# Splitting the transposed residual at the layer borders: four scaled blocks kept in fp32, then one rounding and one remainder over 512 columns

## The chip, the cores and the metric

The kernel runs on one core of a Trainium2 chip. The core has a matrix engine (TensorE, PE in the rows, with PEld for its weight loads), VectorE (DVE), ScalarE (ACT), GpSimd (POOL) and a queue engine that issues the DMAs (SP). Each engine works through its own list of instructions in order, and waits on semaphores of the others. The metric is the device time of one execution in microseconds; a change of under about 0.2% can't be told from none.

## The reference

Two transformer stacks, one after the other, on 256 tokens of width 1024, all in fp32. What matters here is the frame: each layer normalises the residual `x`, multiplies it by learned weights `g`, and feeds it to large matrix products.

```python
def rmsnorm(x, g, eps):                       # g: (1024,)
    return x * rsqrt(mean(x * x, -1) + eps) * g

for layer in range(2):                        # first block
    x = x + mixer(rmsnorm(x, ln1_g[layer])) @ w_o[layer]          # three attention mixers
    x = x + square(relu(rmsnorm(x, ln2_g[layer]) @ w_up[layer])) @ w_down[layer]
x = rmsnorm(x, final_g)
for i in range(4):                            # second block: retention, conformer, short conv, retention
    h = mixer_i(rmsnorm(x, norm_g[i, 0]))
    x = x + rmsnorm(h, norm_g[i, 1])
    h = square(relu(rmsnorm(x, norm_g[i, 2]) @ w1[i])) @ w2[i]
    x = x + rmsnorm(h, norm_g[i, 3])
```

Retention also multiplies its gated output by weights `ret_gn_g` before `ret_w_out`.

## The kernel before

All 256 tokens stay on chip as two tiles `x0` and `x1` of 128 tokens by 1024 (called token half 0 and 1 below). Weights stream in by DMA, 512 KB at a time, into `raw` buffers. To multiply with near-fp32 precision, each operand is split in two parts of the type fp32r: `hi`, the value rounded to fp32r by ScalarE, and `lo`, the remainder `value - hi` by VectorE. A product then is three matmuls: hi·hi, hi·lo, lo·hi. For weights these parts are `whi` and `wlo` (a 128x1024 cast on ScalarE and a 128x1024 subtraction on VectorE for each 512 KB). For the activations they are tiles named `t4k` in the rows.

A *border* is the place between one sub-layer and the next: six mixers and six MLPs give eleven borders, and the input adds one at the start. At a border the class `Pre` takes the new residual. `Pre.split` (line 661) transposes four 128x128 blocks of `x` on TensorE into one PSUM bank (`ps<-ident,x` in the rows) and calls `split_scaled` (line 905), which makes the hi and lo parts of `x` transposed times `g`. `g` lies along the partitions there, so each of the four blocks has its own column of the tile `cv`, and ScalarE's scale takes one column at a time. A border calls `split_scaled` four times: two token halves by two column halves of 512. The retention mixer calls it too, eight times in each of its two layers (`do_g`, twice for each of four heads). That makes 12 × 4 + 16 = 64 calls.

After a border the next sub-layer's first products run in a special order (`lagged`, line 814): with the order `LAG`, token half 0 first, its 16 matmuls with hi over all eight blocks, then its 8 with lo, then the same 24 for token half 1. Before the border, `tail` (line 883) finishes the last products of token half 0 ahead of those of token half 1, so that the residual of half 0 can be finished while TensorE still works on half 1.

The program is first recorded and then put in order by a list scheduler (`Rec.schedule`, line 411): each engine takes, among the instructions whose inputs its cost figures hold ready, the one with the earliest due time, and the due times are counted back from TensorE's order. So a change in one helper moves instructions on every engine near it. The order so found is the order that each engine then keeps on the chip. In the trace all instructions have one line (L563), and go by the names of their tiles.

Of the kernel before, what the change touches and what calls it, by code (L numbers as in the profile page):

```python
# [15 lines left out]
AF = mybir.ActivationFunctionType  # L16
ALU = mybir.AluOpType

P = 128
# [680 lines left out]
class Net:  # L700
# [204 lines left out]
    def split_scaled(self, pt, hi, lo, t, col):  # L905
        nc = self.nc
        ts_ = slice(t * P, (t + 1) * P)
        bs = [(b, self.cv[:, col + b:col + b + 1], pt[:, b * P:(b + 1) * P]) for b in range(4)]
        for b, g, src in bs:
            nc.scalar.activation(hi[:, b, ts_], src, AF.Copy, scale=g)  # L910
        for b, g, src in bs:
            nc.vector.scalar_tensor_tensor(lo[:, b, ts_], src, g, hi[:, b, ts_], op0=ALU.mult, op1=ALU.subtract)

    def evac(self, dst, src):
        self.flip ^= 1
# [863 lines left out]
```

## Time and profile before

| | |
|---|---|
| runs | 1937.51 us median of 3 (1935.68 to 1938.13) |
| profiled execution | 1934.96 us, its span 1933.2 us |
| TensorE busy | 1894.6 us (98%), mean granted clock 0.992 |
| VectorE busy | 1696.6 us (88%), 2895 instructions |
| ScalarE busy | 1249.6 us (65%), 2165 instructions |
| GpSimd busy | 155.6 us (8%) |

The span is from the first to the last instruction; 1.8 us of the profiled execution lie around it. Busy time is the union of an engine's instructions. Matmuls overlap in TensorE's pipeline: one with 512 columns is listed with some 0.39 us, while the next starts 0.23 us after it. The mean of one ScalarE or VectorE instruction also holds an overlap with the next one of about 0.1 us.

### The profile page before, as it was taken

What the parts mean: (1) busy time and instruction counts of PE and PEld (TensorE: products, weight loads), DVE (VectorE), ACT (ScalarE), POOL (GpSimd) and SP (SyncE); (2) the same over time, 40 slices, a digit from 0 to 9 for tenths busy, and PEclk for the clock granted to TensorE, in tenths of its full rate; (3) what the DMA queues carried; (4) which work ended last, traced back from release to release, by engine and by line L of the source; (5) the groups of instructions that cost most, each with busy time, mean ns of one, the idle gap of its engine ahead of it and who ended that gap; (6) DMA issues with size and microseconds to landing.
All of it is one profiled execution on the core that took longest, in us unless ns stands there. A gap on an engine that the chain in (4) does not pass through costs nothing.

```text
span 1933.2 us, 31326 instructions
## 1 busy us (share of the span) xinstructions
PE 1894.6 (98%) x11444; PEld 1675.7 (87%) x11444; DVE 1696.6 (88%) x2895; ACT 1249.6 (65%) x2165; POOL 155.6 (8%) x233
## 2 busy tenths in 40 slices
PE   8999999999999999999998899999999999999998
PEld 7989998888997888899978789979899889888997
DVE  7879999789999776699989899987799987758998
ACT  7557776557776335577679677664676753546775
POOL 2200002110001000000039300000000010000000
PEclk9999999999999999999999899999999999999999
DMA  6345656244565555455642456656456655553563
GB/s 232 113 151 179 210 199 201 77 156 162 198 223 204 180 173 181 135 184 198 229 137 102 131 167 208 208 181 220 135 190 217 208 197 171 169 183 131 192 212 120
DMA packets 95771, 341.49 MB, mean 177 GB/s; under 512 B 10624, under 2 KB 10880, under 8 KB 95616
## 3 DMA queue, kind: packets, MB, share of 16 engines
q1 hardware_dynamic: 95616, 339.49, 52.9%
q8 instruction: 89, 1.46, 0.3%
q14 instruction: 66, 0.54, 0.1%
HBM read 338.40 MB, written 1.05 MB: 176 GB/s over the span
## 4 chain that ended last, share of the span: by engine, by line
PE 90%; DVE 5%; ACT 2%; issue 1%; DMA 1%; POOL 1%; DVEq 0%; POOLq 0%; ACTq 0%
PE ps L563 90%; DVE wlo L563 2%; DVE s2k L563 1%; ACT s2k L563 1%; DVE ps L563 1%; POOL col L563 1%; DMA raw<-in_w 1%; DVE x L563 0%; ACT whi L563 0%; DVE raw L563 0%; DVE t4k L563 0%; DMA x<-in_x 0%; DVE r2k L563 0%; DVE s1k L563 0%; ACT t4k L563 0%
## 5 line engine op out<-in xcount | busy, mean ns | idle before, releaser
L563 ACT CAST whi<-raw 128x1024 fp32r<-128x1024 f32 (+2 forms) x807 | 779.8, 991 | 424.6 <-PE ps L563 237.8
L563 DVE TENSOR_TENSOR wlo<-raw,whi 128x1024 fp32r<-128x1024 f32 (+2 forms) x807 | 913.2, 1156 | 126.2 <-ACT whi L563 122.2
L563 PE MATMUL ps<-whi,t4k 128*128 128x512 f32 (+2 forms) x2808 | 882.0, 392 | 8.4 <-ACT t4k L563 6.7
L563 PE MATMUL ps<-t4k,whi 128*128 128x256 f32 x3712 | 661.9, 282 | 0.0
L563 PEld LDWEIGHTS ps<-whi,t4k 128*128 128x128 f32 x2808 | 523.2, 189 | 115.3 <-ACT t4k L563 9.0
L563 PEld LDWEIGHTS ps<-t4k,whi 128*128 128x128 f32 x3712 | 571.6, 188 | 8.9
L563 PE MATMUL ps<-wlo,t4k 128*128 128x512 f32 (+2 forms) x1404 | 532.3, 392 | 0.0
L563 PE MATMUL ps<-t4k,wlo 128*128 128x256 f32 x1856 | 510.4, 281 | 0.0
L563 PEld LDWEIGHTS ps<-t4k,wlo 128*128 128x128 f32 x1856 | 345.0, 189 | 0.1
L563 PEld LDWEIGHTS ps<-wlo,t4k 128*128 128x128 f32 x1404 | 265.4, 190 | 48.3 <-DVE wlo L563 0.4
L563 DVE TENSOR_TENSOR raw<-raw,raw 128x1024 f32<-128x1024 f32 (+1 forms) x168 | 159.3, 948 | 0.4
L563 POOL TENSOR_TENSOR col<-col,mhalf 128x1 f32<-128x1 f32 (+1 forms) x48 | 43.5, 915 | 1137.9 <-DVE col L563 1137.6
L563 ACT ACTIVATE s2k<-ps 128x512 f32<-128x512 f32 (+2 forms) x116 | 67.2, 582 | 88.6 <-PE ps L563 87.8
L563 DVE TENSOR_TENSOR t4k<-s2k,t4k 128x512 fp32r<-128x512 f32 (+1 forms) x172 | 106.0, 616 | 6.4 <-ACT t4k L563 6.1
L563 ACT CAST t4k<-s2k 128x512 fp32r<-128x512 f32 (+1 forms) x172 | 97.0, 564 | 2.3 <-DVE s2k L563 1.3
L563 ACT ACTIVATE s2k<-s2k 128x512 f32<-128x512 f32 (+1 forms) x118 | 73.9, 627 | 27.5 <-DVE s2k L563 27.1
L563 PE MATMUL ps<-s2k,s2k 128*128 128x64 f32 (+6 forms) x492 | 85.1, 309 | 6.6 <-DVE s1k L563 6.0
L563 PEld LDWEIGHTS ps<-s2k,s2k 128*128 128x128 f32 (+2 forms) x492 | 72.0, 198 | 18.3 <-DVE s1k L563 6.4
L563 PE MATMUL ps<-whi,r2k 128*128 128x512 f32 x288 | 85.4, 395 | 0.2 <-DVE s2k L563 0.2
L563 DVE SCALAR_TENSOR_TENSOR t4k<-ps,cv,t4k 128x128 fp32r<-128x128 f32 x256 | 72.0, 342 | 11.7 <-ACT t4k L563 11.5
L563 ACT ACTIVATE t4k<-ps,cv 128x128 fp32r<-128x128 f32 x256 | 71.4, 378 | 13.0 <-PE ps L563 8.2
L563 DVE TENSOR_TENSOR s2k<-s2k,s2k 128x128 f32<-128x128 f32 (+1 forms) x200 | 68.4, 346 | 3.7 <-ACT s2k L563 3.7
(119 smaller groups left out, 1276.4 us busy)
## 6 DMA issues: line engine op xcount, KB each, us to landing
raw<-in_w SPq DMA_DIRECT2D x599, 512.0 KB, 4.2
raw<-in_w SPq DMA_DIRECT2D x26, 384.0 KB, 3.6
row<-in_rows SPq DMA_DIRECT2D x11, 512.0 KB, 5.8
raw<-in_w SPq DMA_DIRECT2D x8, 288.0 KB, 3.0
raw<-in_w SPq DMA_DIRECT2D x4, 432.0 KB, 7.0
kcs<-in_kc SPq DMA_DIRECT2D x2, 768.0 KB, 7.8
x<-in_x SPq DMA_DIRECT2D x4, 256.0 KB, 6.1
out_dram<-x SPq DMA_DIRECT2D x4, 256.0 KB, 2.0
```

The lines of the kernel that those rows point to most:

```text
L563: op.dma = fn(*[res(a) for a in op.args], **{k: res(a) for k, a in op.kw.items()})
```

## The change

`split_scaled` is the only function changed. ScalarE's four scaled copies go into a new fp32 tile `w` in SBUF (128x512, tag `s2k`) instead of rounding straight into `hi`. Then the existing helper `hilo` makes both parts: one ScalarE cast of 512 columns rounds `w` into `hi`, and one VectorE subtraction of 512 columns writes `w - hi` into `lo`. Before, VectorE formed the remainder by four instructions that each read the PSUM block, `g` and `hi`.

```diff
@@ split_scaled
         bs = [(b, self.cv[:, col + b:col + b + 1], pt[:, b * P:(b + 1) * P]) for b in range(4)]
+        w = self.t("s2k", [P, 4, P])
         for b, g, src in bs:
-            nc.scalar.activation(hi[:, b, ts_], src, AF.Copy, scale=g)
-        for b, g, src in bs:
-            nc.vector.scalar_tensor_tensor(lo[:, b, ts_], src, g, hi[:, b, ts_], op0=ALU.mult, op1=ALU.subtract)
+            nc.scalar.activation(w[:, b, :], src, AF.Copy, scale=g)
+        self.hilo(hi[:, :, ts_], lo[:, :, ts_], w)
```

```python
    def hilo(self, hi, lo, src):
        self.nc.scalar.copy(hi, src)
        self.nc.vector.tensor_sub(lo, src, hi)
```

The first place is ScalarE's order at the border from the second MLP to the first retention layer, token half 0. Before (`ps_330` and `ps_174` hold the transposed column halves, `t4k_181` and `t4k_122` are their hi parts, `s2k<-x` are sums of squares):

```order
L563 ACTIVATE s2k_116,col_163<-x_65 128x512
L563 ACTIVATE s2k_410,col_282<-x_65 128x512
L563 ACTIVATE t4k_181<-ps_330,cv 128x128 x4
L563 ACTIVATE t4k_122<-ps_174,cv 128x128 x4
L563 CAST whi_127<-raw_98 128x1024
```

ScalarE's order at the same place in the change (`s2k_89` and `s2k_168` are the new fp32 tiles, `t4k_190` and `t4k_1519` the hi parts):

```order
L563 ACTIVATE s2k_89,col_266<-x_65 128x512
L563 ACTIVATE s2k_168,col_578<-x_65 128x512
L563 ACTIVATE s2k_89<-ps_139,cv 128x128 x4
L563 ACTIVATE s2k_168<-ps_165,cv 128x128
L563 CAST t4k_190<-s2k_89 128x4x128
L563 ACTIVATE s2k_168<-ps_165,cv 128x128 x3
L563 CAST whi_347<-raw_96 128x1024
L563 CAST t4k_1519<-s2k_168 128x4x128
```

Each column half's hi part is now written by a cast after its four copies, and the cast of the first stands behind the first copy of the second.

The second place is TensorE's order at the border from the first retention mixer to its MLP, around the transposes of token half 1 (`x_65`). Before (`ps_114` collects half 0's first products, with lo parts in `t4k_129` and `t4k_122`; `ps_330` collects those of half 1, with hi part `t4k_337`):

```order
L563 MATMUL ps_483<-ident,x_65 128x128 x4
L563 MATMUL ps_114<-whi_613,t4k_129 128x512
L563 MATMUL ps_174<-ident,x_65 128x128 x4
L563 MATMUL ps_114<-whi_613,t4k_129 128x512
L563 MATMUL ps_114<-whi_520,t4k_129 128x512 x2
L563 MATMUL ps_114<-whi_266,t4k_122 128x512 x2
L563 MATMUL ps_114<-whi_155,t4k_122 128x512 x2
L563 MATMUL ps_330<-whi_613,t4k_337 128x512
```

TensorE's order there in the change (half 0 in `ps_320`, half 1 in `ps_451` with hi part `t4k_332`):

```order
L563 MATMUL ps_320<-whi_194,t4k_341 128x512 x2
L563 MATMUL ps_320<-whi_126,t4k_341 128x512 x2
L563 MATMUL ps_320<-whi_531,t4k_196 128x512
L563 MATMUL ps_451<-ident,x_65 128x128 x4
L563 MATMUL ps_320<-whi_531,t4k_196 128x512
L563 MATMUL ps_175<-ident,x_65 128x128 x4
L563 MATMUL ps_320<-whi_251,t4k_196 128x512 x2
L563 MATMUL ps_451<-whi_194,t4k_332 128x512
```

Between the last transposes and half 1's first product stood seven matmuls, and there now stand two.

## Rows read from the trace of the kernel before

**Rows 1.** The page: busy time of each engine, then the chain by engine.
```profile
PE 1894.6 (98%) x11444; PEld 1675.7 (87%) x11444; DVE 1696.6 (88%) x2895; ACT 1249.6 (65%) x2165; POOL 155.6 (8%) x233
...
PE 90%; DVE 5%; ACT 2%; issue 1%; DMA 1%; POOL 1%; DVEq 0%; POOLq 0%; ACTq 0%
```

**Rows 2.** Waits of all engines: waiting engine and its output, releaser: total us, times, longest.
```profile
PE ps L563 <- DVE s1k L563: 6.9, 2, 6.0
...
PE ps L563 <- ACT t4k L563: 6.7, 5, 1.9
...
PEld ps L563 <- DVE wlo L563: 0.4, 1, 0.4
```

**Rows 3.** Timeline, TensorE and ScalarE, MLP to retention: start us, us, what, [idle].
```profile
606.35 1.32 PE L563 MATMUL ps<-ident,x 128*128 128x128 f32 x8 [1.10 <-DVE x L563]
609.59 0.50 PE L563 MATMUL ps<-whi,t4k 128*128 128x512 f32 x1 [1.92 <-ACT t4k L563]
...
609.19 2.14 ACT L563 ACTIVATE t4k<-ps,cv 128x128 fp32r<-128x128 f32 x8
```

**Rows 4.** Timeline, TensorE and ScalarE: MLP to conformer, then MLP to short conv.
```profile
986.31 0.80 PE L563 MATMUL ps<-whi,t4k 128*128 128x512 f32 x1 [1.62 <-ACT t4k L563]
...
1285.68 0.80 PE L563 MATMUL ps<-whi,t4k 128*128 128x512 f32 x1 [1.16 <-ACT t4k L563]
```

**Rows 5.** Timeline, ScalarE and TensorE, MLP to the second retention.
```profile
1556.46 1.64 ACT L563 ACTIVATE t4k<-ps,cv 128x128 fp32r<-128x128 f32 x6
...
1555.19 0.47 PE L563 MATMUL ps<-whi,t4k 128*128 128x512 f32 x1
...
1556.87 0.50 PE L563 MATMUL ps<-whi,t4k 128*128 128x512 f32 x1 [0.51 <-ACT t4k L563]
...
1557.89 0.40 PE L563 MATMUL ps<-whi,t4k 128*128 128x512 f32 x1
```

**Rows 6.** Windows, attention border, retention: stretch, length, PE, PEld, DVE, ACT, POOL, clock.
```profile
125.00:145.00 20.00, 20.00 (x99) 16.33 (x98) 14.99 (x28) 10.84 (x25) 0.00 (x0) 1.00 0.24 81
...
730.00:805.00 75.00, 75.00 (x341) 61.11 (x340) 46.04 (x68) 38.96 (x67) 0.35 (x1) 1.00 0.55 176
```

**Rows 7.** Lines by shape: busy us, mean ns of one, idle before.
```profile
L563 DVE SCALAR_TENSOR_TENSOR t4k<-ps,cv,t4k 128x128 fp32r<-128x128 f32 x256 | 72.0, 342 | 11.7 <-ACT t4k L563 11.5
L563 ACT ACTIVATE t4k<-ps,cv 128x128 fp32r<-128x128 f32 x256 | 71.4, 378 | 13.0 <-PE ps L563 8.2 <-DVE t4k L563 3.6
L563 DVE TENSOR_TENSOR t4k<-s2k,t4k 128x512 fp32r<-128x512 f32 x88 | 60.0, 682 | 6.4 <-ACT t4k L563 6.1
...
L563 ACT CAST t4k<-s2k 128x512 fp32r<-128x512 f32 x88 | 54.1, 615 | 2.1 <-DVE s2k L563 1.3
```

**Rows 8.** Timeline, ScalarE: the first four copies, at the program's start.
```profile
5.50 1.14 ACT L563 ACTIVATE t4k<-ps,cv 128x128 fp32r<-128x128 f32 x4 [0.51 <-PE ps L563]
```

**Rows 9.** Timeline, ScalarE and TensorE, retention to its MLP, token half 1.
```profile
813.68 2.17 ACT L563 ACTIVATE t4k<-ps,cv 128x128 fp32r<-128x128 f32 x8 [1.71 <-DVE t4k L563]
...
813.05 0.60 PE L563 MATMUL ps<-ident,x 128*128 128x128 f32 x4
...
813.72 0.60 PE L563 MATMUL ps<-ident,x 128*128 128x128 f32 x4
814.08 2.11 PE L563 MATMUL ps<-whi,t4k 128*128 128x512 f32 x8
```

**Rows 10.** Timeline, TensorE, conformer to its MLP; the wait for token half 1.
```profile
1114.69 0.63 PE L563 MATMUL ps<-ident,x 128*128 128x128 f32 x4 [1.14 <-DVE x L563]
```

**Rows 11.** Windows: clock after two waits, clock at 1556, the conformer's convolution.
```profile
610.70:614.10 3.40, 3.40 (x14) 2.66 (x13) 3.40 (x11) 3.40 (x11) 0.39 (x1) 0.50 0.82 269
...
1283.10:1289.90 6.80, 5.64 (x20) 4.19 (x19) 6.36 (x14) 5.71 (x20) 1.58 (x1) 0.50 0.58 213
...
1556.00:1560.00 4.00, 3.49 (x16) 2.53 (x15) 4.00 (x9) 3.08 (x11) 1.46 (x1) 1.00 0.18 46
...
994.00:1062.00 68.00, 61.54 (x424) 57.23 (x422) 62.18 (x126) 60.87 (x142) 56.60 (x75) 0.97 0.30 101
```

## Prediction

> **What bounds the kernel now.** I read the shares of busy time and the chain that ended last first. TensorE is busy 98% of the span and makes 90% of the chain; VectorE, at 88%, makes 5% [rows 1]. So time can be lost or won only where TensorE stands still, and I went on to the waits. TensorE waits for hi parts of activations (`t4k` from ScalarE) five times, 6.7 us in all. Its weight loads wait for `wlo`, VectorE's main product, once, for 0.4 us; the longest wait for VectorE is one of 6.0 us, inside the conformer, at a tile named `s1k` that the change doesn't touch [rows 2]. VectorE is full but runs ahead of TensorE almost everywhere.
>
> Then the timelines of the borders. They fall into three kinds. At the four borders from an MLP to a retention, conformer or short-conv mixer TensorE has nothing to do between the transposes and the first product: it waits 1.92 us at 609.59 and restarts 0.40 us after ScalarE's first copy at 609.19, since the first product needs one block of hi alone [rows 3]; at two others it waits 1.62 and 1.16 us [rows 4]; at the fourth it starts early with four matmuls on two blocks, waits 0.51 us and goes on [rows 5]. At the borders from a mixer to its MLP, TensorE has products of token half 0 left while half 1's hi parts are made. At the three attention borders and in the retention mixers' interior it has more than enough: 20.00 of 20.00 us and 75.00 of 75.00 us busy [rows 6].
>
> **The change part by part.** Engine time first. Of the 256 remainders on VectorE, 72.0 us go; 64 subtractions of 0.682 us, 43.6 us, come: -28.4 us. ScalarE keeps its 256 copies, now to fp32, which I cost the same, and gets 64 casts of 0.615 us: +39.4 us [rows 7]. ScalarE is busy 65% [rows 1], so nothing follows from its sum alone; on DMAs and on GpSimd the change puts nothing, and no row shows TensorE waiting there at these places. The new tile takes a buffer from `s2k`'s pool; I cost that at nothing, because at these places the pool's other users have finished, and half a microsecond at most per border if not, about one cast.
>
> [...]
>
> Now the delay of hi. Before, the first product could start 0.40 us after the first copy. In the order of the change the cast stands behind the four copies and the first copy of the other column half, so five copies at 0.25 us each (four take 1.14 us, the last of them about 0.38, hence 0.25 from start to start [rows 7, 8]), then 0.615 us of cast, and 0.06 us for two handovers: 1.93 us. So hi of the first half comes 1.5 us later, and nothing of it can be used before.
>
> Uncovered borders: at 609, 986 and 1285 that is 1.5 us each, 4.5 us. At 1556 ScalarE has made two copies early and starts the other six at 1556.46; three of these come ahead of the cast, so hi is ready at 1556.46 + 0.75 + 0.615 + 0.05 = 1557.88. By then TensorE has now done eight matmuls, four from 1555.19 and four from 1556.87; the ninth starts at 1557.89 [rows 5]. Eight times 0.23 us is 1.9 us that now come after. Sum 6.4 us.
>
> Half-covered borders, retention to its MLP: ScalarE starts when the transposes of half 1 at 813.05 end, at 813.68 [rows 9], and hi comes 1.93 us later, at about 815.6. In the new order TensorE has left from 813.65 on only one matmul (0.23 us), the second four transposes (0.36 us, from 813.72 to 814.08 [rows 9]) and two matmuls, in sum 1.0 us: it waits about 1.0 us. Before, the seven matmuls in that place made the wait none. The second retention's border has the same two matmuls left, 1.0 us; the short conv's has one left instead of five, 1.1 us. Sum 3.1 us. The five matmuls that are missing there are done earlier, in time in which TensorE was busy anyway, so they don't pay the wait back.
>
> Conformer to its MLP: TensorE already waits 1.14 us, for VectorE's `x` [rows 10]. Ahead of that `x` stand eight remainders, now two subtractions: 8 × 0.281 - 2 × 0.682 = 0.9 us [rows 7] that VectorE may give back, against 1.5 us of later hi: between +0.6 and +1.5, taken +1.0. Start of the program: the copies at 5.50 [rows 8] are followed by the first weights' casts on the same engine, so one cast, 0.6 us (bounds 0 and 1.2, two casts). Attention borders and retention's interior: nothing, hidden by products of the other half; without that cover the three borders and sixteen calls would cost 1.5 us each, 28 us, which I leave out, as TensorE shows no gap there [rows 6].
>
> The clock. [...] A stretch of 3.4 us at half the clock holds 1.7 us of work at the full one, so it costs 1.7 us. At 1556, after a wait of 0.72 and then of 0.51 us, the clock stays 1.00. There the stop becomes one of over 2 us in a piece, as long as the one before 609.59, so I expect it to fall: +1.7, but with a chance of some 6 in 10: +1.0. Bounds for all borders: -0.8 each (a stretch that is slow already is in part spent idle) and +1.7 each.
>
> VectorE's relief. 28.4 us less work helps only where TensorE waits on VectorE. By rows 2 the wait on `wlo` is worth 0.4 us. The waits inside the conformer, where VectorE has work for 62.18 of 68 us [rows 11], may shrink by what the border ahead gives back: 16 × 0.281 - 4 × 0.682 = 1.8 us. I take -1.5 in all, with bounds 0 and -6 (1.8 at three borders where VectorE holds up `x`).
>
> Sum: 6.4 + 3.1 + 1.0 + 0.6 + 1.0 - 1.5 = 10.6 us. The profiled execution took 1934.96 us, its span 1933.2 and 1.8 around it; with 10.6 that is 1945.6. The median of the runs shown is 2.55 us above it (1937.51), so 1948 us.
>
> **The rivals.** B, no change: a new order is made for the new instruction lengths, and the stalls are refilled. TensorE's weight parts are ready ahead, so leftover products of the mixer, moved behind the transposes, could hide what I count at 815 and its like; and the four uncovered waits could hide behind casts that stand there anyway. Against it: the order of the change shows fewer such products, not more, and at 609 none are left. It would leave 4.5 us at three borders and take back 1.5 to 4 of it: +2, 1939.5 us.
>
> C, faster: VectorE's backlog decides. For it: 88% busy, and the wait of 6.0 us on `s1k` [rows 2] after a stretch where VectorE is nearly full [rows 11]. Then 1.8 us at each of three borders and 0.9 at the conformer's exit come back, 6.3 us, the delay of hi costs 1 to 2, and the time is 4.5 us shorter, 1933 us. It decides from the point where less than a third of the delay is seen by TensorE. Against it: TensorE's waits at the borders name ScalarE, not VectorE.
>
> D, much slower: each new stop lets the clock fall. At the five borders that hold 1.00 or have no stop now, 1.7 us each are 8.5 us more than the sum less its own 1.0: +18, 1955.5 us. For it: the half clock behind the stops at 610 and 1283 [rows 11]. Against it: the stops of about 1 us at 1114 and 1556 [rows 5, 10] are short.
> [...]
>
> **How the numbers follow.** Forecast (A, +6 to +16, so 1943.5 to 1953.5): 0.60. B 0.17, C 0.11, D 0.12. From 0.2% on, 3.9 us, a measurement of this kernel tells a difference from none. A and D lie above that: slower 0.72; B within: 0.17; C below: faster 0.11. The range leaves out C and what of D lies higher: 1938 to 1957.
>
> **What would show it.** VectorE's busy time near 1668, ScalarE's near 1289, TensorE's nearly unchanged but for half-clock stretches. The stop before the first product grows from 1.92 to about 3.4 us after 609, to about 3.1 and 2.7 at the next two, and names ScalarE's `t4k`; new stops of about 1 us for `t4k` stand at the exits of both retentions and the short conv; at the second retention's entrance a stop of 2 us with a clock of 0.50 behind it. The total of TensorE's waits on ScalarE's `t4k` rises from 6.7 to about 16 us. I am wrong if these stops are there and the time isn't (then waits elsewhere shrank: look at `x` and `s1k`), or if the stops are missing (then hi was not late, or covered).

## The result and the profile after

The changed kernel takes 1953.38 us, the median of 4 runs (1952.55 to 1955.48), against 1936.6 us (1935.07 to 1938.13) for the kernel before: +16.8 us, a ratio of 1.009 with an interval of 1.0076 to 1.0104. It is slower, as forecast, by more than the 10.6 us that the sum gave. The time lies 0.1 us inside the forecast's 1943.5 to 1953.5 us, but the difference lies outside its +6 to +16, as these runs of the kernel before are 0.9 us faster than those that the forecast set out from; that the time came to lie inside is luck. In the outer range, 1938 to 1957, it lies clearly.

The page after, busy times and the chain by engine, answers [rows 1]:

```profile
PE 1897.1 (97%) x11444; PEld 1675.4 (86%) x11444; DVE 1674.4 (86%) x2703; ACT 1285.2 (66%) x2229; POOL 155.5 (8%) x233
...
PE 88%; DVE 6%; ACT 3%; issue 2%; POOL 1%; DMA 0%; SPq 0%; DVEq 0%; POOLq 0%; ACTq 0%
```

VectorE lost 22.2 us of work (28.4 forecast), ScalarE gained 35.6 (39.4), and TensorE 2.5 only. The span of this trace is 17.6 us longer, so 15.1 us are in TensorE's stops. Its waits, as in [rows 2] (waiting engine and output, releaser, total us, times, longest):

```profile
PE ps L563 <- ACT t4k L563: 19.6, 10, 3.5
PE ps L563 <- DVE s1k L563: 6.7, 1, 6.7
PE ps L563 <- DVE x L563: 6.0, 5, 2.0
```

The wait for hi parts is three times what it was (6.7 us), twice as often; the two longest groups of waits for VectorE have hardly moved, 22 us less work or not (6.9 and 6.7 us before; those for `s2k` rose from 3.7 to 5.1).

The entrance to the first retention mixer, TensorE and then ScalarE, answers [rows 3]:

```profile
608.51 1.32 PE L563 MATMUL ps<-ident,x 128*128 128x128 f32 x8 [1.11 <-DVE x L563]
613.28 0.80 PE L563 MATMUL ps<-whi,t4k 128*128 128x512 f32 x1 [3.45 <-ACT t4k L563]
...
611.35 1.37 ACT L563 ACTIVATE s2k<-ps,cv 128x128 f32<-128x128 f32 x5
612.60 0.63 ACT L563 CAST t4k<-s2k 128x512 fp32r<-128x512 f32 x1
```

Five copies, then the cast, then the product: 1.93 us from the first copy to the product, where it was 0.40. The stop is 3.45 us where it was 1.92.

The entrances to conformer, short conv and second retention, TensorE's lines, answer [rows 4, 5]:

```profile
991.38 0.79 PE L563 MATMUL ps<-whi,t4k 128*128 128x512 f32 x1 [2.28 <-ACT t4k L563]
...
1297.15 0.80 PE L563 MATMUL ps<-whi,t4k 128*128 128x512 f32 x1 [3.15 <-ACT t4k L563]
...
1570.61 0.79 PE L563 MATMUL ps<-whi,t4k 128*128 128x512 f32 x1 [2.71 <-ACT t4k L563]
```

The four stops have grown by 1.53, 0.66, 1.99 and 2.20 us, 6.4 us together. From the first of the transposes to the first product behind the stop it is 1.5, 0.9, 1.5 and 1.0 us longer than before.

The exits of first retention (here with the matmuls ahead), short conv and second retention; before, no wait for hi stood there (the five of [rows 2] are the four at the entrances and one of 1.46 us inside the conformer):

```profile
818.10 0.60 PE L563 MATMUL ps<-ident,x 128*128 128x128 f32 x4
818.45 0.70 PE L563 MATMUL ps<-whi,t4k 128*128 128x512 f32 x2
820.02 0.51 PE L563 MATMUL ps<-whi,t4k 128*128 128x512 f32 x1 [0.87 <-ACT t4k L563]
...
1400.29 0.51 PE L563 MATMUL ps<-whi,t4k 128*128 128x512 f32 x1 [1.33 <-ACT t4k L563]
...
1778.55 0.50 PE L563 MATMUL ps<-whi,t4k 128*128 128x512 f32 x1 [0.86 <-ACT t4k L563]
```

Three new stops, 3.1 us together.

Windows (stretch, length, busy of PE, PEld, DVE, ACT, POOL, clock), behind the stops at the entrances to conformer and second retention:

```profile
988.40:995.20 6.80, 4.52 (x15) 3.16 (x14) 6.36 (x12) 5.87 (x19) 2.60 (x3) 0.50 0.01 2
1568.70:1575.50 6.80, 4.89 (x16) 4.11 (x17) 6.36 (x10) 5.73 (x19) 2.06 (x1) 0.50 0.25 83
```

At a granted clock of 0.50 for 6.8 us each. Before, the first was a stretch of 3.4 us and the second didn't exist (clock 1.00 at 1556, [rows 11]).

Where the loss builds up is seen by laying the two traces on one another at the first transposes of `x` of each border. Extra time of each stretch in us, in the changed kernel and in four of the experiments below (single traces, each against the one of before; a stretch whose lists are those of before shows up to 0.9 in these columns, and in the traces of two other runs 1.5 and 2.3):

| stretch | change | four entrances | second retention | conformer | lists held |
|---|---|---|---|---|---|
| first transposes to the first attention mixer's exit | +1.7 | 0.0 | -0.3 | -0.3 | +4.8 |
| on to the first retention mixer's entrance | +0.6 | -0.1 | 0.0 | +0.2 | +0.2 |
| first retention | +1.1 | +1.3 | +0.9 | -0.1 | +1.8 |
| its MLP | +0.9 | -0.2 | 0.0 | 0.0 | +1.8 |
| conformer | +4.5 | +5.0 | +0.1 | +2.1 | +3.2 |
| its MLP | +1.3 | 0.0 | +0.1 | 0.0 | +3.0 |
| short conv | +1.2 | +0.7 | 0.0 | -0.3 | +2.7 |
| its MLP | +1.6 | -0.1 | 0.0 | +0.1 | +3.0 |
| second retention | +4.5 | +4.3 | +4.2 | 0.0 | +3.2 |
| its MLP | +0.4 | -0.6 | -0.7 | -0.7 | +1.7 |

Two rows carry half of it: the conformer and the second retention. They are what the sum had too small. They are not alike. The conformer's stage in windows, before and after:

```profile
983.37:1100.03 116.66, 102.41 (x619) 91.54 (x620) 104.82 (x222) 92.65 (x226) 74.41 (x107) 0.91 0.31 102
987.52:1108.64 121.12, 102.52 (x618) 90.44 (x619) 105.24 (x210) 94.84 (x228) 73.63 (x106) 0.90 0.30 103
```

TensorE is busy as long as before, 102.5 us, and stands still 4.4 us longer: 0.7 at the entrance, 0.1 at the wait for `x` just ahead of it, and 3.6 inside the conformer. In the second retention, of 4.5 us, 2.2 are waiting and 2.3 are longer busy time, with the half clock in it:

```profile
1553.84:1750.57 196.73, 196.18 (x1067) 167.93 (x1067) 140.65 (x225) 92.08 (x147) 7.33 (x12) 1.00 0.54 175
1566.58:1767.80 201.22, 198.50 (x1067) 169.89 (x1067) 136.30 (x189) 98.63 (x159) 7.94 (x12) 0.98 0.53 171
```

### The profile page after: what moved, and what is told of

It is laid out like the page before. It is cut to its first block, busy times and chain, and to the rows that moved or that the text cites. A ratio compares the mean times of both kernels' runs of the same rounds, so it can differ in the third digit from the quotient of the medians.

```text
span 1950.8 us, 31223 instructions
## 1 busy us (share of the span) xinstructions
PE 1897.1 (97%) x11444; PEld 1675.4 (86%) x11444; DVE 1674.4 (86%) x2703; ACT 1285.2 (66%) x2229; POOL 155.5 (8%) x233
## 3 DMA queue, kind: packets, MB, share of 16 engines
q8 instruction: 89, 1.46, 0.3%
## 4 chain that ended last, share of the span: by engine, by line
PE 88%; DVE 6%; ACT 3%; issue 2%; POOL 1%; DMA 0%; SPq 0%; DVEq 0%; POOLq 0%; ACTq 0%
PE ps L563 88%; DVE wlo L563 3%; ACT s2k L563 1%; DVE s2k L563 1%; DVE raw L563 1%; DVE ps L563 0%; ACT whi L563 0%; DMA x<-in_x 0%; POOL col L563 0%; ACT t4k L563 0%; POOL s1k L563 0%; DVE x L563 0%; ACT s1k L563 0%; DVE r2k L563 0%; DVE t4k L563 0%
## 5 line engine op out<-in xcount | busy, mean ns | idle before, releaser
L563 PE MATMUL ps<-whi,t4k 128*128 128x512 f32 (+2 forms) x2808 | 883.7, 392 | 19.6 <-ACT t4k L563 19.6
L563 DVE TENSOR_TENSOR t4k<-s2k,t4k 128x384 fp32r<-128x384 f32 (+1 forms) x236 | 150.2, 638 | 24.1 <-ACT t4k L563 24.0
L563 ACT CAST t4k<-s2k 128x384 fp32r<-128x384 f32 (+1 forms) x236 | 137.8, 584 | 2.3 <-DVE s2k L563 1.1
L563 ACT ACTIVATE s2k<-ps,cv 128x128 f32<-128x128 f32 x272 | 81.1, 386 | 14.2 <-PE ps L563 12.6
L563 POOL TENSOR_TENSOR s1k<-s1k,s1k 128x256 f32<-128x256 f32 (+1 forms) x97 | 64.2, 692 | 12.1 <-ACT s1k L563 11.5
```

The source lines that it names most:

```text
L563: op.dma = fn(*[res(a) for a in op.args], **{k: res(a) for k, a in op.kw.items()})
```

## The experiments

The theory to test, L: the time comes from the later hi part, at the borders where TensorE has nothing else, by the stop itself and the half clock behind it. Its rivals: the larger load of ScalarE, the reordering of the lists, or simply each call's share.

**Hi early, lo in one piece.** The four rounding copies are back, four more copies fill the fp32 tile, and VectorE subtracts once over 512 columns.

```diff
         for b, g, src in bs:
-            nc.scalar.activation(w[:, b, :], src, AF.Copy, scale=g)
-        self.hilo(hi[:, :, ts_], lo[:, :, ts_], w)
+            nc.scalar.activation(hi[:, b, ts_], src, AF.Copy, scale=g)
+        for b, g, src in bs:
+            nc.scalar.activation(w[:, b, :], src, AF.Copy, scale=g)
+        nc.vector.tensor_sub(lo[:, :, ts_], w, hi[:, :, ts_])
```

> ScalarE writes hi from the transposed blocks in four scaled copies as before, then writes the four scaled blocks once more into the fp32 tile, and VectorE makes lo in one subtraction of 512 columns as in the change. So hi is early again while VectorE's 28 us of relief and ScalarE's longer list (64 x 1.1 us = 71 us more than before, more than the change's 39) both stay. Theory L (the late hi part costs the time): 0 to +4 us against before, and the stops for t4k at the MLP-to-mixer borders are again about 1.2 to 2 us. Rival E (ScalarE's larger load or the new order of the lists costs the time): +10 us or more. Rival V (without the delay VectorE's relief shows): -4 us or less.

1936.89 us against 1934.87 us, ratio 1.0011 (1.0002 to 1.002): +2.0 us. The waits for hi are those of before again, and ScalarE is loaded more than in either kernel; the page of this kernel, and its wait:

```profile
PE 1897.5 (98%) x11444; PEld 1675.4 (87%) x11444; DVE 1672.5 (86%) x2703; ACT 1311.7 (68%) x2421; POOL 155.4 (8%) x233
```
```profile
PE ps L563 <- ACT t4k L563: 5.8, 4, 2.1
```

ScalarE has 62 us more work than before, more than in the change, and nearly the whole loss is gone. So it isn't ScalarE's load, nor a new order as such (this kernel has one of its own), and VectorE's relief, 24 us here, brought nothing that can be seen; whether ScalarE's extra work ate a gain of VectorE's can't be told apart here.

**Borders only, gated output only, four entrances only.** The change is made where a condition on the border's row of weights holds, the old body elsewhere: `row is not None` for the borders only, `row is None` for the retention mixers' interior, and for the four entrances

```diff
+        if row in ("n0_0", "n1_0", "n2_0", "n3_0"):
+            w = self.t("s2k", [P, 4, P])
...
+        else:
+            for b, g, src in bs:
+                nc.scalar.activation(hi[:, b, ts_], src, AF.Copy, scale=g)
...
```

> The change in the 48 calls at the borders only; the 16 calls inside the two retention mixers as before. Theory L: the interior is covered by other products, so all of the loss stays: +15 to +18 us. Rival R (each call counts alike): 48 of 64 of 16.8 us, +12.6 us.

> The change in the 16 calls inside the retention mixers only. Theory L: -1 to +1 us, TensorE busy without a gap there. Rival R: 16 of 64 of 16.8 us, +4.2 us.

> The change at the four borders from an MLP to a retention, conformer or short-conv mixer only (16 of 64 calls). By the distance from border to border in the two traces these four stages took 1.05 + 4.47 + 1.19 + 4.49 = 11.2 us more. Theory L: +9 to +13 us, with a half clock behind the stop at the second retention as in the change. Rival O (much of it comes from the reordering that the other calls bring): +4 to +7 us (1.5 us for each border).

Borders only: 1951.03 us, 1.0081 (1.0068 to 1.0093), +16.2 us. Interior only: 1936.33 us, 1.0005 (0.9996 to 1.0014), +1.5 us, a little above the -1 to +1 expected and not told from zero. Four entrances only: 1944.31 us, 1.0046 (1.0034 to 1.0059), +9.4 us, all against 1934.87 us. A quarter of the calls makes more than half of the loss, another quarter none: it is not the call that costs but its place. Rival R (each call alike) falls, and the cover of the interior holds.

**The second retention alone, and with filler.** First the change at that border only (`row == "n3_0"`). Then the same with transposes that nobody reads, issued behind the eight of token half 0:

```diff
         net.split_scaled(pt, self.xt[hf][0], self.xt[hf][1], t, CV[self.row] + 4 * hf, self.row)
+        if self.row in ('n3_0',) and t == 0 and hf == 1:
+            pf = net.ps()
+            for _ in range(22):
+                nc.tensor.transpose(pf[:, :P], src[:, :P], net.ident)
```

> The change in the four calls at the border to the second retention only. Theory L with the clock: the stage took 4.49 us more in the changed kernel, eight first matmuls held back (1.9 us) and a half clock of 6.8 us behind the stop; so +3.5 to +5 us here with the rest unchanged. Rival O (the half clock there came from what other borders moved): +1.5 to +2 us, clock 1.00 behind the stop.

> As the kernel before it (the change at the border to the second retention only), with 22 further transposes of 128 columns behind the eight of token half 0, whose output nobody reads: they fill TensorE's stop of 2.7 us without shortening it. If the clock's fall behind the stop is what the stop costs beyond its own length: clock 1.00 there and +1 to +2 us against before, some 2.5 to 3.4 less than without the filler. Rival (the length of the stop alone counts): the same as without the filler, +4 or more.

Without filler 1939.25 us, 1.0019 (1.0011 to 1.0028), +3.9 us; with filler 1936.43 us, 1.0005 (0.9997 to 1.0014), +1.1 us, both against 1935.35 us. TensorE at the stop, without filler and the window behind it:

```profile
1553.88 1.32 PE L563 MATMUL ps<-ident,x 128*128 128x128 f32 x8 [0.72 <-DVE x L563]
1557.93 0.80 PE L563 MATMUL ps<-whi,t4k 128*128 128x512 f32 x1 [2.73 <-ACT t4k L563]
```
```profile
1556.20:1563.00 6.80, 5.07 (x16) 4.21 (x17) 6.36 (x10) 6.55 (x22) 2.06 (x1) 0.50 0.23 84
```

and with filler:

```profile
1553.78 3.72 PE L563 MATMUL ps<-ident,x 128*128 128x128 f32 x30 [0.72 <-DVE x L563]
1557.83 0.50 PE L563 MATMUL ps<-whi,t4k 128*128 128x512 f32 x1 [0.33 <-ACT t4k L563]
```
```profile
1556.20:1563.00 6.80, 6.47 (x38) 5.28 (x37) 6.36 (x9) 6.56 (x22) 2.06 (x1) 1.00 0.22 83
```

The first product starts as late in both, 2.7 us behind the border's own transposes. With the stop filled the clock stays at 1.00. So 2.8 of the 3.9 us (2.0 to 4.0 by resampling the eleven runs of each) are the half clock, and the lateness by itself is worth 1.1, not told from zero. By the two traces' stretches, +4.2 and +1.9 us, it is 2.3 and 1.9. The clock is half of this border's price or more.

**The conformer alone** (`row == "n1_0"`).

> The change in the four calls at the border to the conformer only. The stage took 4.47 us more in the changed kernel, while the stop at its entrance grew by 0.8 us only. Theory L (late entrance, one more window of half clock, later work in the conformer's chain of ScalarE and VectorE): +4 to +5 us, no other stage moved. Rival O (the reordering by the other calls, the exit to the MLP among them): +1 to +2 us.

1935.53 us against 1935.35 us, 1.0004 (0.9995 to 1.0013): no loss that can be measured; the single trace has the stage 2.1 us longer. Its entrance stops longer than in the changed kernel:

```profile
986.92 0.79 PE L563 MATMUL ps<-whi,t4k 128*128 128x512 f32 x1 [3.16 <-ACT t4k L563]
```

So theory L misses here: this border's own price is 0 to 2 us, and the 4.5 us of the conformer in the change, 5.0 with four entrances changed, need the others too. What the others change there is the order of the lists, and the traces bear that out. Counted as above (TensorE's idle time in the stage, less what the entrance's stop and the wait for `x` grew by), the waits inside the conformer are 3.6 us longer in the change, 3.4 with the borders only, whose lists in this stage are the same as the change's on every engine, 2.6 with the four entrances, and 0.6 with the conformer alone. In three runs whose lists here are those of before (interior only, second retention, filler) they are 0 to 1.2 us longer. In the trace of the change, waits stand inside the conformer that before hadn't or had shorter (TensorE, MLP of the conformer not included):

```profile
1054.19 0.70 PE L563 MATMUL ps<-s2k,raw 128*128 128x256 f32 x2 [0.80 <-DVE s2k L563]
...
1060.20 1.99 PE L563 MATMUL ps<-s2k,raw 128*128 128x256 f32 x8 [0.73 <-DVE raw L563]
...
1082.02 0.30 PE L563 MATMUL ps<-ident,s1k 128*128 128x128 f32 x1 [2.43 <-ACT whi L563]
```

The last was 0.98 us before, for VectorE's `s1k`; it was 2.02 in the run with filler, with the lists of before. These waits are on work that the change doesn't touch.

**Copies first, in the kernel before.** At the entrance, sums of squares and a weight cast stand on ScalarE between the transposes (606.35) and the copies (609.19, [rows 3]). Here the scheduler is told that the copies, and VectorE's remainders with them, are due 4 us earlier.

```diff
         for op in ops:
             if op.rush and op.eng in ("sync", "scalar") and op.name != "copy":
                 op.dl = op.i - 1e9
+            op.dl -= op.early
...
+        net.rec.early = 4000.0
         net.split_scaled(pt, self.xt[hf][0], self.xt[hf][1], t, CV[self.row] + 4 * hf)
+        net.rec.early = 0.0
```

> The kernel before, with the due time of ScalarE's scaled copies at the borders set 4 us earlier, so that they stand ahead of the sums of squares and the weight cast that come between the transposes and them (about 1.5 us at the borders to the first retention, the conformer, the short conv and the second retention). If hi's time is what TensorE waits for: stops of 0.4 to 0.8 us in place of 1.2 to 1.9, -4 to -8 us against before, more where the half clock goes too. Rival (the sums and the cast that are now later hold up something else): no gain, -1 to +2 us.

1927.3 us against 1935.35 us, 0.9958 (0.9946 to 0.9971): -8.0 us, faster than both kernels. TensorE's and ScalarE's lines at the first retention's entrance:

```profile
608.45 0.47 PE L566 MATMUL ps<-whi,t4k 128*128 128x512 f32 x1 [0.76 <-ACT t4k L566]
...
610.90 0.50 PE L566 MATMUL ps<-whi,t4k 128*128 128x512 f32 x1 [0.84 <-ACT t4k L566]
...
607.98 0.88 ACT L566 ACTIVATE t4k<-ps,cv 128x128 fp32r<-128x128 f32 x3
```
```profile
606.00:614.00 8.00, 6.03 (x30) 4.43 (x31) 8.00 (x17) 7.51 (x21) 1.47 (x1) 1.00 0.69 229
```

One stop of 1.92 us has become two of 0.8, and the clock doesn't fall behind either. In the whole trace, up to the last products, the granted clock is 0.50 for 17.1 us, 30.7 before and 41.0 in the change. Of the 7.3 us that this trace is shorter, 4.0 are busy time of TensorE and 3.4 waiting. The lists moved elsewhere too, most in the conformer, so the gain is that of the whole new order.

**The change with the lists held.** All engines keep the order of the kernel before; only the instructions of `split_scaled` are exchanged. The old body is recorded and put in order; `swap`, a new function, then turns the four rounding copies into copies to `w`, puts the cast behind the fourth, and a subtraction in the place of the fourth remainder.

```diff
-        order = self.rec.schedule()
+        order = self.rec.swap(self.rec.schedule(), 2)
```

> The whole change, but every engine keeps the order of the kernel before: the four copies stand where the four rounding copies stood, the cast directly behind the fourth, the subtraction where the fourth remainder stood. TensorE's list is that of before, so seven matmuls cover half 1's hi at the exits of the retention mixers again. Theory L with a share for the order: entrances +1.3 us each at three borders, 1.7 and 1.7 to 3.4 of half clock at the second retention, 1.7 of half clock at the conformer, 1 us at the start and 1 at the conformer's exit, none at the exits and none inside the conformer: +8 to +12 us. Rival O (most of the loss is the reordering): +2 to +6 us. Rival P (the order has no part in it): +15 to +18 us.

1960.4 us against 1935.38 us, 1.013 (1.0115 to 1.0145): +25.0 us. All three numbers missed. One reason stands at the start, where 4.8 of the 25 us arise (ScalarE, then TensorE):

```profile
9.53 0.88 ACT L662 ACTIVATE s2k<-ps,cv 128x128 f32<-128x128 f32 x3 [0.95 <-PE ps L662]
10.30 1.05 ACT L662 CAST whi<-raw 128x1024 fp32r<-128x1024 f32 x1
11.23 0.65 ACT L662 ACTIVATE s2k<-x 128x512 f32<-128x512 f32 x1
...
11.86 0.37 ACT L662 ACTIVATE s2k<-ps,cv 128x128 f32<-128x128 f32 x1
12.26 0.62 ACT L662 CAST t4k<-s2k 128x512 fp32r<-128x512 f32 x1
...
12.93 0.80 PE L662 MATMUL ps<-whi,t4k 128*128 128x512 f32 x1 [2.63 <-ACT t4k L662]
```

The old order may put a weight cast and a sum between the third and the fourth copy, because the old first product needs the first block alone. The cast needs all four, and TensorE stops for 2.63 us at 12.93. At the entrances to first retention and conformer the four copies and the cast stand together, so this isn't the reason there. The stretches that begin at the four exits (the MLP rows of the table) cost 1.7 to 3.0 us each, and TensorE's waits for `x`, 6.7 us in 5 before, have grown in number:

```profile
PE ps L662 <- DVE x L662: 9.9, 8, 1.9
```

Why those grew is not shown. So the scheduler's new order isn't a cost of the change over all: held in this way, the old one costs 8 us more. It is in the conformer's interior that the old order is better: there its longest waits are 5.96, 1.50 and 3.46 us, as before but for 0.5 us.

**The change with copies first, and with the cast kept close.** The first is the edit of the copies above, in the changed kernel (copies, cast and subtraction due 4 us earlier). The other two runs let the cast follow the copies at once in the scheduler's figures, where it held a result of ScalarE for ready on ScalarE only 0.131 us later; once without, once with the earlier due times.

```diff
-                q.est = max(q.est, op.end + (700.0 if op.dma else latency(e, q.eng)))
+                near = op.tight is not None and op.tight == q.tight and q.eng == e == "scalar"
+                q.est = max(q.est, op.end + (700.0 if op.dma else 0.0 if near else latency(e, q.eng)))
```

> The changed kernel with the due time of the four copies and of the cast at the borders 4 us earlier, as in the experiment that put the copies first in the kernel before (-8.0 us). Theory L: the copies and the cast start about 1.5 us earlier at the entrances and the cast's delay stays, so it lands 8 to 14 us above that one, near the kernel before: 0 to +6 us. Rival (once the sums and the weight cast stand behind, the delay is covered): -6 us or less.

> The changed kernel; in the scheduler's figures alone, the cast may follow the four copies that it reads at once instead of 0.131 us later, in which gap another instruction of ScalarE's list slips in between. Theory S (what slips in delays hi beyond the cast itself): 0.25 us less at each uncovered border and some of what the order cost in the conformer, +10 to +15 us against before. Rival (the cast and the wait for all four blocks are the whole delay): +16 to +18 us, as the change.

> The changed kernel with the copies and the cast 4 us earlier in due time and the cast directly behind its copies. Theory S: here a sum of squares (0.64 us) or a weight cast (1.03 us) stood between the copies and the cast, so the stops at the entrances get 0.6 to 1 us shorter each and some half clock goes: +6 to +14 us against before. If the delay of the cast were cheap once it stands early and alone: 0 us or below. Rival (what slips in has no part): +18 to +21 us as without it.

Copies first: 1955.17 us against 1935.38 us, 1.0097 (1.008 to 1.0114), +19.8 us, above every number expected. Cast close: 1952.66 us, 1.0087 (1.0073 to 1.0101), +17.5 us. Both: 1946.17 us, 1.0055 (1.0043 to 1.0068), +11.1 us, these two against 1935.11 us. ScalarE at the first retention's entrance, copies first, without and then with the cast kept close:

```profile
609.03 1.14 ACT L566 ACTIVATE s2k<-ps,cv 128x128 f32<-128x128 f32 x4
610.04 0.64 ACT L566 ACTIVATE s2k<-x 128x512 f32<-128x512 f32 x1
...
610.65 0.63 ACT L566 CAST t4k<-s2k 128x512 fp32r<-128x512 f32 x1
```
```profile
609.75 1.14 ACT L569 ACTIVATE s2k<-ps,cv 128x128 f32<-128x128 f32 x4
610.92 0.62 ACT L569 CAST t4k<-s2k 128x512 fp32r<-128x512 f32 x1
```

A sum of 0.64 us slips between the copies and the cast, and goes when the gap goes; with the copies first that is worth over 8 us over the program, in the range of theory S. Its way there is shown only in part: the first stops at the four entrances are 0.2 to 0.8 us shorter, 1.6 together, where 0.6 to 1 each was expected, and the time at half the clock falls from 51.2 to 37.5 us. Nor is the slipped sum all that is wrong with copies first alone: its conformer takes 8.6 us more than before, with waits of 8.70 and 5.08 us for `s1k` (5.96 and 0.98 before), on work that the change doesn't touch.

```profile
1070.80 5.21 PE L566 MATMUL ps<-s2k,s2k 128*128 128x128 f32 x30 [8.70 <-DVE s1k L566]
...
1084.98 0.48 PE L566 MATMUL ps<-ident,s1k 128*128 128x128 f32 x1 [5.08 <-DVE s1k L566]
```

Without the earlier due times the gap let in one copy of 0.25 us at that entrance, and closing it gains nothing measurable: there the rival's number holds. Closing it could not gain much: the cast starts 0.50 us behind the start of the last copy that it reads with the first of the next half between, and 0.40 us with nothing between. And the change still costs in the best place tried: with the same due times the kernel without the change stands 8.0 us below the kernel before, and the one with it 11.1 us above, each against its own runs of the kernel before.

## Why the prediction came out as it did

The direction and the mechanism were right; the size of the sum, 10.6 us against 16.8, was off in four of its terms.

| term of the sum | forecast | measured |
|---|---|---|
| longer stops at the four entrances | 6.4 | 6.4, from the stops |
| new stops at three exits | 3.1 | 3.1, from the stops |
| conformer to its MLP | 1.0 | 1.3, from the stretch |
| start of the program | 0.6 | 1.7, from the stretch |
| half clock | 1.0 | 2.3, from the second retention's busy time (2.8 by the filler) |
| VectorE's relief, in the main inside the conformer | -1.5 | +3.6, waits inside the conformer |

The measured terms come to 18.4 us, against 17.6 in the traces. They can't be added up to the last tenth: where a stretch was slow already, part of a longer stop falls into it (the first retention's stop grew by 1.53 us, its stretch by 1.1).

**Stops.** Cast behind five copies, 1.93 us from first copy to product: measured 1.93. Sum of the entrances and of the exits as forecast, though not border by border: the conformer's grew by 0.66 and the short conv's by 1.99 us where each was to grow by 1.5. At the conformer one sum of squares had moved ahead of the transposes, so that the copies start 1.9 us behind the first transpose instead of 2.5; at the short conv the first product comes 1.5 us later, as forecast, but the transposes, 1.78 us before, are done in 1.32. That the two even out in the sum is luck. At the second retention hi, which the forecast had ready at 1557.88, lets the first product start, counted from the transposes, at 1557.87. "The total of TensorE's waits on ScalarE's `t4k` rises from 6.7 to about 16 us": to 19.6, with 2.31 at the start and 1.13 at the conformer's exit (where a wait of 1.14 us for `x` stood before).

**Inside the conformer.** This is the term that was off most. The prediction took the conformer's waits to shrink, since VectorE is nearly full there and would be relieved, and put -1.5 us for that, with nothing above 0 in its bounds; they grew by 3.6. It had priced the delay of hi at the borders, and a new order only where it covers a stop, not what a new order does to waits on work that the change leaves alone.

**Clock.** It was named, placed right (a stop of over 2 us, measured 2.71, and a clock of 0.50 behind it) and priced, from the 3.4 us at 0.50 in [rows 11], at 1.7 us with 6 chances in 10. The fall came, and lasted 6.8 us, not 3.4: 2.8 us by the pair with and without filler. The prediction had a stretch of 6.8 us in its rows too, at 1283, and took the shorter one. At the conformer's entrance the slow stretch doubled as well, from 3.4 us before to 6.8, which the busy time of its stage doesn't show (102.41 and 102.52 us). The window of before there, and one of the kernel changed at the second retention only, behind the first retention's entrance, where the lists are those of before:

```profile
986.20:989.60 3.40, 3.29 (x8) 2.65 (x9) 2.96 (x7) 2.69 (x10) 2.10 (x2) 0.50 0.05 18
...
607.30:614.10 6.80, 5.53 (x17) 4.65 (x18) 6.80 (x14) 6.65 (x23) 1.47 (x1) 0.50 0.53 187
```

In the second, the same stop of 1.92 us as in [rows 3] is followed by 6.8 us at half the clock, where [rows 11] has 3.4, and the stretch is 0.9 us longer. So 3.4 or 6.8 behind a stop isn't a matter of its length alone, and which it would be was not to be read from one trace.

The filler shows the same fall from the other side: with 22 transposes in the same wait the granted clock stayed at 1.00, where without them it was 0.50 for 6.8 us.

Rival D had the clock fall at five more borders. It fell at one new one; the stops of 0.86 to 1.33 us at the exits left it at 1.00.

**Start.** The cast stands behind a weight cast of 0.63 us, and the next weight cast behind it. ScalarE's lines in the change are

```profile
5.43 1.14 ACT L563 ACTIVATE s2k<-ps,cv 128x128 f32<-128x128 f32 x4 [0.57 <-ACT s2k L563]
6.44 0.63 ACT L563 CAST whi<-raw 128x512 fp32r<-128x512 f32 x1
6.95 0.65 ACT L563 CAST t4k<-s2k 128x512 fp32r<-128x512 f32 x1
7.47 0.64 ACT L563 CAST whi<-raw 128x512 fp32r<-128x512 f32 x1
```

TensorE's first stop is 2.31 us where it was 1.74 (for a weight cast), so the 0.6 that was forecast is right for it. The rest of the stretch's 1.7 is in no term: a wait of 0.71 us for the DMA of `x` and one of 0.68 for `s2k` at 39.00, which before weren't there.

**VectorE's relief.** "28.4 us less work helps only where TensorE waits on VectorE" was right, and -1.5 us was too much. Rival C, faster by the freed time, would have shown in the kernel with hi early and lo in one piece, and that one is 2.0 us slower than before, unless ScalarE's 62 us more ate the gain.
On VectorE one subtraction of 687 ns stands where four remainders of 342 stood (these also read PSUM). The end time doesn't follow from it: TensorE's two longest groups of waits for VectorE, 6.9 and 6.7 us before, are 6.7 and 6.0 in the change.

**Rival B**, that a new order refills the stalls: half right. Against the lists as held here reordering saved 8 us of 25. The forecast read the new order at the borders and so had what it does there in its numbers, but not what it does inside the conformer.

**Open.** Of the conformer's 4.5 us, 3.6 are waits inside it, for `s2k`, `raw`, `s1k` and a weight cast, and in no term of the sum. They come with the new order of the lists: the borders-only kernel has the same order there and 3.4 us, changing the conformer's own entrance alone gives 0.6, and holding the lists leaves 1.0. Which of the other borders moves the lists so was not separated, and a trace with the lists of before can show 1.2 us too. Which waits made the held lists 8 us worse is shown at the start only. And no run shows alone what VectorE's relief is worth with ScalarE's load unchanged.

## What to carry over

When small instructions are merged into one large one, ask what the first reader needed: here one block of 128 columns let the next product start after 0.40 us, and the merged rounding made it wait for all four, 1.93 us. Busy time saved on an engine that nobody waits for is no gain: VectorE's 24 us, with hi early, brought nothing that can be seen. What an uncovered stop of TensorE costs need not be its length alone: behind the stop of 2.73 us at the second retention the granted clock was 0.50 for 6.8 us, and that was half of this border's price or more; over the whole change 15 of 17.6 us were waiting. And where a scheduler orders everything anew, look at the waits on work that the change leaves alone: inside the conformer they were 3.6 us. Before making an instruction cheaper at such a place, look at what stands ahead of it in its queue: making the same copies due ahead of the sums and the weight cast gained 8 us, with the same instructions in another order.

## What the runs showed of the hardware

A wait of 2.73 us (second retention alone) was followed by 6.8 us at a granted clock of 0.50, and with 22 unread transposes in the same wait the clock was 1.00 there, a gain of 2.8 us. Two waits of 0.76 and 0.84 us, 2.45 us apart from start to start of the products behind them (copies first), left it at 1.00, and so did those of 0.86 to 1.33 us at the exits in the change. Behind one and the same stop of 1.92 us the clock was 0.50 for 3.4 us in one trace (before) and for 6.8 in another (second retention alone).

On ScalarE, a cast that reads what ScalarE just wrote started 0.40 to 0.41 us after the start of the last copy (131.28 and 131.69, the change; 11.86 and 12.26 with the lists held), 0.03 us after that copy's end; a cast that doesn't read the copy in front started 0.25 us after its start (612.35 and 612.60, the change). By these two numbers a cast directly behind its copies costs some 0.16 us more, near the 0.131 us of the scheduler's figures; one copy of 0.25 us let into that gap then costs some 0.09 us (the cast 0.50 us behind the start of the last copy that it reads, against 0.41).
